# Neighbourhood attention on 8-column query tiles, with values and gates projected partly beside the head that uses them

## The chip, the cores and the metric

One core of one Trainium2 chip runs the whole program in one launch. The metric is the device time of that launch in microseconds (us), as the median of several runs. The engines are named as in the profile: PE is the matrix engine (PEld its weight loads, which overlap its products), DVE the vector engine, ACT the scalar engine, POOL the engine that here casts weights and issues the accumulating DMAs, SP the engine that issues the other DMAs.

## What is computed

A two-layer encoder on 1024 prompt tokens (16 rows x 64 columns) and 256 sample tokens (4 x 64), width 1024, in float32. The change touches only layer 0, the neighbourhood attention:

```python
proj = h @ w_in                                   # h: RMS-normed tokens
q, k, v, g = jnp.split(proj, 4, axis=-1)          # 16 heads of 64
# a query (r, c) sees 8 rows x 16 columns of keys around it; the window is
# clamped at the edges of the grid, and a per-head 2-D bias is added
s = jnp.where(mask, s + bias, NEG_INF)
p = jax.nn.softmax(s, axis=-1)
o = p @ v
return (o * jax.nn.silu(g)) @ w_out
```

Layer 1 (a gated DeltaNet) and the final norm follow, and are the same in both kernels.

## The kernel before

The tokens of the prompt are kept column after column: token index = 16 * column + row, so eight columns are 128 tokens, called a strip. Every product of float32 numbers that has to be exact is made of rounded parts: `wh` and `wl` are the high and the low part of a weight, `XH` and `XL` of the input, `KH` and `KL` of the keys, `ph` and `pl` of the probabilities. A projection is 24 products for each block of tokens (8 steps of the width, three pairs of parts; line 1108), with blocks of 512, 512 and 256 tokens. Values are projected token-major, by strip, with 24 products of 256 columns each (line 1124).

Per head h, `attention` is a generator that emits the head's steps. The prompt is cut into four tiles j of 16 columns (256 queries). In a tile, the queries are split by rows into two groups of 8 rows x 16 columns, and each group is scored against 12 key rows x 32 columns = 384 keys (`ROWS`, `SLAB`). The scores of one group are two products of 384 columns into `S` (lines 279 and 280). `softmax` (lines 224 to 227) adds the bias and takes the extreme (DVE), exponentiates and sums (ACT), takes the reciprocal and scales (DVE). The probabilities stand in tiles of 16 rows x 32 columns in which the four unseen key rows are zeros. `pv` turns them, four 128x128 transposes for two strips (line 238), rounds them to `ph` (ACT, line 241) and `pl` (DVE, line 242), and multiplies each of the four strips of values with 256 query columns, once for `ph` and once for `pl` (line 254). Lines 259 to 261 gate the result into `O`. The sample is a fifth tile with two strips.

So one head makes per prompt tile 4 score products of 384 columns, 8 transposes (4 strips x 2 groups) and 8 value products of 256 columns (4 strips x 2 parts). With the sample that is 20 score products, 36 transposes and 36 value products.

While head h is in `attention`, the projections for the next head run beside it. `Side` holds the order, written out by hand: every projection product advances a clock by its columns (`tick`), and a generator is stepped when the clock has passed the delay that it last yielded; `until` steps it without the clock until a condition holds, and `drain` empties it. The scheduler of the language keeps this as the priority, and may put a later instruction that is ready ahead of one that isn't. Beside head h run the query and key projection of head h + 1 (`qk_head`), after an odd head also the gates of the next two heads (`g_pair`, 3 blocks), and after every fourth head the values of the next four heads (`v_quad`, 10 strips). The loop is

```python
side.add(attention(h, qkk, V, G, O), 8000)
if h < 15:
    qkk = qk_head(h + 1, side)
    if h % 2:     G = g_pair((h + 1) // 2, side)
    if h % 4 == 3: V = v_quad((h + 1) // 4, side)
side.drain()
```

Weights pass through one raw buffer and three buffers each for `wh` and `wl` (`load_w`): a load by SP, a cast on POOL, a negated copy on ACT, and an accumulating DMA issued by POOL. The bias is loaded by SP, three times 384 KB for each head into two buffers. The PSUM banks are three for projections, two for `S`, two for `pt` (the transposes) and one for `O` of line 254. After head 15 the out-projection reads the heads' outputs back from memory.

Of the kernel before, what the change touches and what calls it, by code (L numbers as in the profile page):

```python
# [8 lines left out]
F32 = mybir.dt.float32  # L9
# [11 lines left out]
SLAB = [0, 8, 24, 32]  # L21
ROWS = [(0, 12), (4, 12)]
# [14 lines left out]
def layer0(ctx, tc, a, h1_out):  # L37
# [77 lines left out]
    def v_quad(q, side):  # L115
        nonlocal wv
        wv = load_v(tc, a, q)
        V = {}
        for s in range(10):
            side.until(lambda: done[4 * q - 1] > (0, 1, 1, 2, 3, 3, 3, 3, 4, 4)[s])  # L120
            V[s] = v_strip(s, token_major(s, side))
        return V

# [51 lines left out]
    with st:  # L175
# [5 lines left out]
        def qk_head(h, side=None):  # L181
# [4 lines left out]
            for b, (t0, n) in enumerate(BLK):  # L186
# [5 lines left out]
                if t0 < NP:  # L192
                    qv = Q[:, :NP].rearrange("p (g c r) -> p c g r", g=2, r=8)[:, t0 // 16:t0 // 16 + 32]
                    tq = t.rearrange("p (c g r) -> p c g r", g=2, r=8)
                else:
                    qv, tq = Q[:, c], t[:, :n]
                nc.scalar.activation(qv[0:64], tq[0:64], AF.Copy)
                nc.scalar.activation(KH[64:128, c], t[64:128, :n], AF.Copy, scale=0.125)
                nc.vector.tensor_sub(qv[64:128], tq[0:64], qv[0:64])
# [6 lines left out]
        def g_pair(p, side=None):  # L206
            wh, wl = load_w(tc, a, a["w_g"][p])
            G = []
            for b, (t0, n) in enumerate(BLK):
# [3 lines left out]
                proj(nc, ps, wh, wl, XH, XL, b, side)  # L213
                t = ap.tile([128, 512], F32, name="t", bufs=2)[:, :n]
                nc.vector.tensor_mul(t, ps, rb[:, t0:t0 + n])
                G.append(ap.tile([128, n], F32, name=f"G{b}"))
                nc.scalar.activation(G[b], t, AF.Tanh, scale=0.5)
                nc.vector.scalar_tensor_tensor(G[b], G[b], 1.0, t, op0=OP.add, op1=OP.mult)
            return G
# [9 lines left out]
        def pv(strips, hh, Od, Gv, t1v):  # L229

            O = ps_o.tile([128, 256], F32, name="O")
            ns = len(strips)

            def turned(s0):
                pt = ps_t.tile([128, 2, 256], F32, name="pt")
                for u in range(2):
                    for g in range(2):
                        nc.tensor.transpose(pt[:, u, 128 * g:128 * g + 128], strips[s0 + u][1][g], ident)  # L238
                ph = ap.tile([128, 2, 256], F32R, name="ph", bufs=2)
                pl = ap.tile([128, 2, 256], F32R, name="pl", bufs=2)  # L240
                nc.scalar.activation(ph, pt, AF.Copy)
                nc.vector.tensor_sub(pl, pt, ph)
                return ph, pl

            ts = []
            for s0 in range(0, ns, 2):
                ts.append(turned(s0))
                yield 800
            for s0 in range(0, ns, 2):
                ph, pl = ts[s0 // 2]  # L250
                for i, p in enumerate((ph, pl)):
                    for u in range(2):
                        v = strips[s0 + u][0][:, hh, :, :].rearrange("p a b -> p (a b)")
                        nc.tensor.matmul(O, v, p[:, u, :], start=(s0 + u + i == 0), stop=(s0 + u + i == ns))  # L254
                    yield 800
# [5 lines left out]
            nc.vector.tensor_mul(Od[b:b + 64], t1v(t1)[b:b + 64], Gv[b:b + 64])  # L261

        def attention(h, qkk, V, G, O):
            Q, KH, KL = qkk
            g3 = lambda t: t[:, :NP].rearrange("p (c r) -> p c r", r=16)
            g4 = lambda t, j: t[:, 256 * j:256 * j + 256].rearrange("p (c g r) -> p g c r", g=2, r=8)
            bts = {}

            def scores(j):
                if j != 2:  # L270
                    bts[j] = ap.tile([128, 768], F32, name="bias", bufs=2)
                    nc.sync.dma_start(bts[j], a["bias_p"][h, (0, 1, 1, 2)[j]])
                bt = bts[1 if j == 2 else j]
                s0 = SLAB[j]
                Pt = []
                for g, (r0, nr) in enumerate(ROWS):
                    S = ps_s.tile([128, 512], F32, name="S")[:, :nr * 32]
                    q = Q[:, 512 * g + 128 * j:512 * g + 128 * j + 128]
                    nc.tensor.matmul(S, q, g3(KH)[:, s0:s0 + 32, r0:r0 + nr], start=True, stop=False)
                    nc.tensor.matmul(S, q, g3(KL)[:, s0:s0 + 32, r0:r0 + nr], start=False, stop=True)  # L280
                    p = P[g][j % 2]
                    b = bt[:, 384 * g:384 * g + 384]
                    cr = lambda v: v.rearrange("p (c r) -> p c r", c=32)
                    softmax(cr(S), cr(b), p[:, :, r0:r0 + nr])
                    Pt.append(p)
                    yield 800
                strips = [(V[s0 // 8 + s], [p[:, 8 * s:8 * s + 8, :].rearrange("p c r -> p (c r)") for p in Pt])
                          for s in range(4)]
# [1068 lines left out]
```

## Time and profile before

| | |
|---|---|
| median of 3 runs | 2426.49 us (2420.15 to 2427.59) |
| the profiled execution | 2429.32 us, span 2427.6 us |
| PE busy | 2281.3 us, 94% of the span |
| PEld, DVE, ACT, POOL busy | 81%, 68%, 51%, 23% |
| granted PE clock, mean | 0.964 |
| first scores of head 0 to the end of head 15's attention | 80.8 to 707.2 us |

The busy time of an engine is a share of the span; the products overlap in PE's pipeline, so a product's duration in a row is longer than the time by which it delays the next one. That time is read from the starts of successive products. The stages behind 707 us (the rest of the out-projection, the DeltaNet, its out-projection and the last norm) are the same code in both kernels.

### The profile page before, as it was taken

Reading aid. Unit: us, or ns where it says so; the run is one execution under the profiler, and the core shown is the slowest. Engines: PE = TensorE matmul, PEld = TensorE weight load, DVE = VectorE, ACT = ScalarE, POOL = GpSimd, SP = SyncE. Lnnn points to the kernel's source line nnn. Section 1 sums busy time; section 2 is a strip of 40 time slices with the busy share of each in tenths; the row PEclk is TensorE's granted clock in tenths of the full one; section 3 lists DMA queues with packets and bytes.
Section 4 is the critical chain, followed back from the end, with each engine's and each line's share of the span. In section 5 each row is a group of like instructions: output and inputs, shape, how many; then the busy total and the mean of one; then the engine's idle time right before and its main releaser. Section 6 shows DMA issues by size and latency. Waiting matters only on the chain.

```text
span 2427.6 us, 37431 instructions
## 1 busy us (share of the span) xinstructions
PE 2281.3 (94%) x13462; PEld 1977.7 (81%) x13462; DVE 1642.4 (68%) x3858; ACT 1241.4 (51%) x2772; POOL 568.6 (23%) x666
## 2 busy tenths in 40 slices
PE   8999999999999698999999999999998899887996
PEld 7889888889778588888988989888777777676886
DVE  5674874784773677867868678694788888843233
ACT  6553553554662543444344443444777777754333
POOL 2000101001110521232223222233444444310100
PEclk9999999999999798989999999999999999988998
DMA  6452534443564333424443444435343334467762
GB/s 182 111 126 75 136 106 105 120 117 89 169 179 135 85 89 95 120 78 120 119 121 85 114 120 119 121 77 160 97 112 104 104 107 117 147 187 225 169 166 87
DMA packets 154649, 297.07 MB, mean 122 GB/s; under 512 B 46304, under 2 KB 83168, under 8 KB 154464
## 3 DMA queue, kind: packets, MB, share of 16 engines
q1 hardware_dynamic: 137760, 233.86, 31.5%
q0 software_dynamic: 16704, 60.82, 13.8%
q8 instruction: 106, 1.74, 0.3%
q14 instruction: 79, 0.65, 0.1%
HBM read 219.26 MB, written 64.88 MB: 117 GB/s over the span
## 4 chain that ended last, share of the span: by engine, by line
PE 63%; DVE 19%; issue 9%; DMA 5%; ACT 3%; POOL 1%; SPq 1%; DVEq 0%; ACTq 0%; POOLq 0%
PE mm L1108 26%; PE mm L1124 11%; PE O L254 3%; DVE X L564 3%; DVE tmp L562 3%; PE k L864 2%; PE k L873 2%; PE pt L238 2%; DVE acc L447 2%; PE u L839 2%; PE o L839 2%; PE o L884 2%; DMA wl<-w_go 1%; PE m L590 1%; PE S L280 1%
## 5 line engine op out<-in xcount | busy, mean ns | idle before, releaser
L1108 PE MATMUL mm<-xh,wh 128*128 128x512 f32 (+1 forms) x1536 | 560.0, 365 | 6.6 <-ACT wh L1060 5.9
L1108 PE MATMUL mm<-xh,wl 128*128 128x512 f32 (+1 forms) x1536 | 557.5, 363 | 6.1 <-DMA wl<-w_qkv 2.5
L1108 PE MATMUL mm<-xl,wh 128*128 128x512 f32 (+1 forms) x1536 | 562.2, 366 | 0.0
L1108 PEld LDWEIGHTS mm<-xh,wh 128*128 128x128 f32 x1536 | 295.3, 192 | 38.4 <-ACT wh L1060 6.4
L1108 PEld LDWEIGHTS mm<-xh,wl 128*128 128x128 f32 x1536 | 294.8, 192 | 37.8 <-DMA wl<-w_qkv 2.7
L1108 PEld LDWEIGHTS mm<-xl,wh 128*128 128x128 f32 x1536 | 295.4, 192 | 29.8 <-issue 0.5
L1124 PE MATMUL mm<-wh,xh 128*128 128x256 f32 x960 | 281.5, 294 | 4.4 <-DVE z L473 4.4
L1124 PE MATMUL mm<-wl,xh 128*128 128x256 f32 x960 | 281.4, 293 | 0.5 <-DVE wl L1062 0.5
L1124 PE MATMUL mm<-wh,xl 128*128 128x256 f32 x960 | 280.2, 292 | 0.3 <-POOL xl L66 0.3
L447 DVE SCALAR_TENSOR_TENSOR acc<-raw,cw,acc 128x1282 f32<-128x1282 f32 x128 | 201.0, 1570 | 61.8 <-ACT acc L445 60.3
L1124 PEld LDWEIGHTS mm<-wh,xh 128*128 128x128 f32 x960 | 187.7, 196 | 9.0 <-DVE z L473 4.8
L1124 PEld LDWEIGHTS mm<-wl,xh 128*128 128x128 f32 x960 | 188.0, 196 | 4.1 <-issue 2.3
L1124 PEld LDWEIGHTS mm<-wh,xl 128*128 128x128 f32 x960 | 187.9, 196 | 3.3 <-issue 1.7
L1108 PE MATMUL mm<-yh,wl 128*128 128x512 f32 (+1 forms) x384 | 143.3, 374 | 27.4 <-DMA wl<-w_go 26.7
L1060 ACT ACTIVATE wh<-wraw 128x1024 fp32r<-128x1024 f32 x94 | 99.1, 1055 | 125.3 <-PE mm L1108 51.8
L1108 PE MATMUL mm<-yh,wh 128*128 128x512 f32 (+1 forms) x384 | 142.1, 371 | 1.7 <-ACT wh L1060 1.7
L1108 PE MATMUL mm<-yl,wh 128*128 128x512 f32 (+1 forms) x384 | 142.5, 372 | 0.1
L1058 POOL CAST wh<-wraw 128x1024 fp32r<-128x1024 f32 x30 | 31.7, 1056 | 472.3 <-PE mm L1108 375.7
L1064 ACT ACTIVATE wl<-wraw 128x1024 fp32r<-128x1024 f32 x116 | 121.9, 1052 | 29.7 <-PE mm L1108 11.4
L860 POOL TENSOR_TENSOR Al<-A,Ah 128x128 fp32r<-128x128 f32 x160 | 76.0, 481 | 175.2 <-ACT Ah L859 163.2
L1108 PEld LDWEIGHTS mm<-yh,wl 128*128 128x128 f32 x384 | 76.7, 200 | 40.2 <-DMA wl<-w_go 28.5
L450 ACT ACTIVATE th<-acc 128x1282 f32<-128x1282 f32 x32 | 40.8, 1275 | 121.0 <-DVE acc L447 121.0
(325 smaller groups left out, 5307.9 us busy)
## 6 DMA issues: line engine op xcount, KB each, us to landing
bias<-bias_p SPq DMA_DIRECT2D x48, 384.0 KB, 3.1
wraw<-w_qkv SPq DMA_DIRECT2D x32, 512.0 KB, 4.2
wl<-w_qkv POOLq DMA_DIRECT2D x32, 512.0 KB, 7.3
qkv_spill<-th SPq DMA_DIRECT2D x32, 512.0 KB, 2.7
wraw<-w_go SPq DMA_DIRECT2D x32, 512.0 KB, 5.9
wl<-w_go POOLq DMA_DIRECT2D x30, 512.0 KB, 7.9
z_spill<-z SPq DMA_DIRECT2D x80, 128.0 KB, 1.7
z<-z_spill SPq DMA_DIRECT2D x80, 128.0 KB, 2.1
```

Source lines behind the costliest of these rows:

```text
L238: nc.tensor.transpose(pt[:, u, 128 * g:128 * g + 128], strips[s0 + u][1][g], ident)
L254: nc.tensor.matmul(O, v, p[:, u, :], start=(s0 + u + i == 0), stop=(s0 + u + i == ns))
L447: nc.vector.scalar_tensor_tensor(acc, r[:, i:i + m], cw[:, f, i:i + 1], acc, op0=OP.mult, op1=OP.add)
L562: nc.vector.tensor_mul(tv, N[:, 0:c, c:c + 1].to_broadcast([128, c, n]), X[:, c:c + 1, c + 1:32].to_broadcast([128, c, n]))
L564: nc.vector.tensor_add(X[:, 0:c, c + 1:32], X[:, 0:c, c + 1:32], tv)
L839: self.tc.nc.tensor.matmul(ps, w[x], v[y], start=(first and i == 0), stop=(i == 2))
L860: nc.gpsimd.tensor_sub(As[d][1], A[:, d, c], As[d][0])
L864: nc.tensor.matmul(pk, kT[:, cc[d]], S[c0, d], start=True, stop=True)
L1060: nc.scalar.activation(wh, raw, AF.Copy)
L1064: nc.scalar.activation(wl, raw, AF.Copy, scale=-1.0)
L1108: nc.tensor.matmul(ps, w[:, k, :], x[k][b], start=(k == 0 and i == 0), stop=(k == KD - 1 and i == 2))
L1124: nc.tensor.matmul(ps, x[k][b][:, cc], w[:, k % 4, :], start=(k == 0 and i == 0), stop=(k == KD - 1 and i == 2))
```

## The change

- A query tile is 8 whole columns (16 rows x 8 columns = 128 queries, one strip), m = 0 to 7. It is scored against the strips m - 1, m and m + 1 with all 16 key rows: 384 keys, 256 for m = 0 and 7. The bias is one table of 896 columns for each head, loaded once (448 KB); the zeros in the probabilities and the strided views are gone.
- Two tiles make a pair (256 queries). Strips m and m + 1 are seen by both tiles and keep products of 256 columns; strips m - 1 and m + 2 are seen by one tile each and get products of 128 columns. A pair in the middle has 6 transposes, one at an edge 5.
- The order of a pair's steps becomes scores of this pair, value products of the pair before, transposes of this pair. Before it was scores of the next tile, transposes of this one, its products.
- The gates and values of the next heads are divided: after an odd head only gate block 0 (after every fourth head also block 1 and the value strips 0 to 3); the rest is projected beside the even head that uses it, before the next `qk_head`. A generator waits in `products` until the gates and strips that it needs have been made.
- Even heads start 2000 columns into the side work instead of 8000, and the delays of a head are multiplied by 1.7, 0.9, 1.15 or 1.7.

The core of the diff:

```diff
-    def v_quad(q, side):
+    def v_quad(q, V, strips, side):
         nonlocal wv
-        wv = load_v(tc, a, q)
-        V = {}
-        for s in range(10):
+        if not V:
+            wv = load_v(tc, a, q)
+        for s in strips:
...
-                if t0 < NP:
-                    qv = Q[:, :NP].rearrange("p (g c r) -> p c g r", g=2, r=8)[:, t0 // 16:t0 // 16 + 32]
...
-                nc.scalar.activation(qv[0:64], tq[0:64], AF.Copy)
+                nc.scalar.activation(Q[0:64, c], t[0:64, :n], AF.Copy)
...
-        def g_pair(p, side=None):
-            wh, wl = load_w(tc, a, a["w_g"][p])
-            G = []
-            for b, (t0, n) in enumerate(BLK):
+        def g_pair(p, G, blocks, side=None):
+            nonlocal wg
+            if not G:
+                wg = load_w(tc, a, a["w_g"][p])
+            for b in blocks:
...
+        def turned(units):
+            ts = []
+            for us in (units[:2], units[2:]):
...
+                for u, parts in enumerate(us):
+                    for s, q0, blocks in parts:
+                        for i, blk in enumerate(blocks):
+                            o = q0 + 128 * i
+                            nc.tensor.transpose(pt[:, u, o:o + 128], blk, ident)
+                            n += 1
...
+                nc.scalar.activation(view(ph), view(pt), AF.Copy)
+                nc.vector.tensor_sub(view(pl), view(pt), view(ph))
...
+        def pv(units, ts, V, hh, Od, Gv):
+            O = ps_o.tile([128, 256], F32, name="O")
+            order = [0, *range(2, len(units)), 1]
+            for i in range(2):
+                for u in order:
+                    p = ts[u // 2][i]
+                    for s, q0, blocks in units[u]:
+                        qs = slice(q0, q0 + 128 * len(blocks))
+                        v = V[s][:, hh, :, :].rearrange("p a b -> p (a b)")
+                        nc.tensor.matmul(O[:, qs], v, p[:, u % 2, qs], start=(i == 0 and u == 0),
+                                         stop=(i == 1 and u == 1))
+                yield 1600
...
+            bt = ap.tile([128, 896], F32, name="bias", bufs=2)
+            nc.sync.dma_start(bt, a["bias_p"][h])
+            def scores(p):
+                own = {}
+                for m in (2 * p, 2 * p + 1):
+                    k0, k1 = max(m - 1, 0), min(m + 2, 8)
+                    n = 128 * (k1 - k0)
+                    S = ps_s.tile([128, 512], F32, name="S")[:, :n]
+                    q = Q[:, 128 * m:128 * m + 128]
+                    nc.tensor.matmul(S, q, KH[:, 128 * k0:128 * k1], start=True, stop=False)
+                    nc.tensor.matmul(S, q, KL[:, 128 * k0:128 * k1], start=False, stop=True)
...
-            todo = yield from scores(0)
-            for j in range(1, 5):
-                after = yield from (scores(j) if j < 4 else scores_s())
-                yield from todo
-                done[h] += 1
-                todo = after
-            yield from todo
+            last = None
+            for j in range(5):
+                units = yield from (scores(j) if j < 4 else scores_s())
+                if last:
+                    yield from products(*last)
+                else:
+                    yield 3200
+                ts = yield from turned(units)
+                last = j, units, ts
+            yield 1600
+            yield from products(*last)
...
-            side.add(attention(h, qkk, V, G, O), 8000)
+            G = nG if h % 2 == 0 else G
+            V = nV if h % 4 == 0 else V
+            side.add(attention(h, qkk, V, G, O), 2000 if h % 2 == 0 else 8000, (1.7, 0.9, 1.15, 1.7)[h % 4])
+            side.tick(0)
+            p, q = (h + 1) // 2, (h + 1) // 4
+            if h % 2 == 0:
+                g_pair(p, G, [b for b in range(3) if b not in G], side)
+                v_quad(q, V, [s for s in range(10) if s not in V], side)
             if h < 15:
...
                 qkk = qk_head(h + 1, side)
-                if h % 2:
-                    G = g_pair((h + 1) // 2, side)
+            if h % 2 and h < 15:
+                nG = {}
+                g_pair(p, nG, [0], side)
                 if h % 4 == 3:
-                    V = v_quad((h + 1) // 4, side)
+                    nV = {}
+                    v_quad(q, nV, range(4), side)
+                    g_pair(p, nG, [1], side)
             side.drain()
```

More of the change, by code (lines that the diff above doesn't have):

```diff
@@ L227, in softmax @@
             nc.vector.tensor_scalar(Pv, Pv, mx[:, 2:3], None, op0=OP.mult)
[L229 to L234, printed above, removed]
+        def turned(units):
+            ts = []
+            for us in (units[:2], units[2:]):
+                if not us:
+                    break
                 pt = ps_t.tile([128, 2, 256], F32, name="pt")
-                for u in range(2):
-                    for g in range(2):
-                        nc.tensor.transpose(pt[:, u, 128 * g:128 * g + 128], strips[s0 + u][1][g], ident)
@@ L239, in turned @@
                 ph = ap.tile([128, 2, 256], F32R, name="ph", bufs=2)
                 pl = ap.tile([128, 2, 256], F32R, name="pl", bufs=2)
[L241 to L247, printed above, removed]
-                yield 800
[L249 to L255, printed above, removed]
+                n = 0
@@ L267, in attention @@
[L267 to L285, printed above, removed]
+            bt = ap.tile([128, 896], F32, name="bias", bufs=2)
@@ new lines, in attention @@
+            nc.sync.dma_start(bt, a["bias_p"][h])
[8 more added lines that the diff above has]
+                    nc.tensor.matmul(S, q, KL[:, 128 * k0:128 * k1], start=False, stop=True)
+                    P = ap.tile([128, 384], F32, name="P", bufs=4)
+                    b0, _ = BIAS[0 if m == 0 else 2 if m == 7 else 1]
+                    softmax(S, bt[:, b0:b0 + n], P[:, :n])
+                    for s in range(k0, k1):
+                        own[s, m] = P[:, 128 * (s - k0):128 * (s - k0) + 128]
@@ L286, in scores @@
                     yield 800
[L287 to L290 removed]
+                m = 2 * p
+                edge = [(s, 128 * i, [own[s, m + i]]) for s, i in ((m - 1, 0), (m + 2, 1)) if (s, m + i) in own]
+                return [[(s, 0, [own[s, m], own[s, m + 1]])] for s in (m, m + 1)] + [edge]
@@ L301, in scores_s, with products @@
                     softmax(S[:, g], bs[:, g], Ps[:, g])
[L302 to L313 removed]
+                yield 1600
+                return [[(8 + s, 0, [Ps[:, g, 128 * s:128 * s + 128] for g in range(2)])] for s in range(2)]
+            def products(j, units, ts):
+                while not (j // 2 in G and all(s in V for us in units for s, _, _ in us)):
+                    yield 400
+                g = G[j // 2][:, 256 * (j % 2):256 * (j % 2) + 256]
+                yield from pv(units, ts, V, h % 4, O[:, 256 * j:256 * j + 256], g)
+                done[h] += 1
+            last = None
[7 more added lines that the diff above has]
+                last = j, units, ts
+            yield 1600
+            yield from products(*last)
             if h % 2 and h < 15:
```

62 lines of the change are left out of this document (25 added, 37 removed).

## The prediction

> **What bounds the kernel now.** I read the page's totals first, then the stretches of the attention stage head by head, then who waits for whom in it, then the order in time on PE. The page says that PE is busy 94% of the span. That is an average; the stretches say it for the stage that is changed (heads 0, 1, 3 and 14, then the whole; the columns are length, busy time of PE, PEld, DVE, ACT and POOL with instruction counts, granted clock, DMA share, GB/s).
>
> ```profile
> span 2427.6 us, 37431 instructions
> 80.80:107.30 26.50, 26.39 (x161) 22.02 (x160) 22.56 (x65) 17.12 (x40) 1.91 (x2) 1.00 0.47 108
> 107.30:149.00 41.70, 41.14 (x241) 34.81 (x240) 29.81 (x78) 20.75 (x47) 3.82 (x4) 1.00 0.47 128
> 175.60:246.10 70.50, 69.94 (x481) 63.60 (x480) 34.60 (x88) 26.54 (x58) 5.73 (x6) 1.00 0.36 94
> 647.80:680.70 32.90, 28.23 (x160) 23.53 (x159) 28.30 (x70) 26.52 (x60) 14.09 (x12) 0.95 0.75 220
> 80.80:707.20 626.40, 615.09 (x3832) 529.53 (x3831) 433.40 (x1163) 330.24 (x741) 65.78 (x66) 1.00 0.46 117
> ```
>
> The heads last from 26.5 to 70.5 us, very uneven, but PE is busy in 98% or more of the first three and of the whole, at the full clock; the light heads have DVE at 22.56 of 26.50 us, high and still behind PE. Head 14, light as head 0, has a hole (28.23 of 32.90). So PE's work is what the stage costs, and a gain is counted in the time by which a product delays the next one, which only the order in time shows:
>
> ```profile
> 81.62 0.34 PE L279 MATMUL S<-KH,Q 128*128 128x384 f32 x1
> 81.80 0.34 PE L280 MATMUL S<-KL,Q 128*128 128x384 f32 x1
> 81.97 0.40 PE L1108 MATMUL mm<-xh,wh 128*128 128x512 f32 x1
> ...
> 84.65 1.00 PE L238 MATMUL pt<-ident,P 128*128 128x128 f32 x7
> 85.41 0.47 PE L1108 MATMUL mm<-xh,wl 128*128 128x512 f32 x1
> 85.72 0.40 PE L1108 MATMUL mm<-xh,wh 128*128 128x512 f32 x1
> 86.01 0.50 PE L254 MATMUL O<-ph,V 128*128 128x256 f32 x2
> 86.35 0.39 PE L1108 MATMUL mm<-xl,wh 128*128 128x512 f32 x1
> 86.58 0.40 PE L1108 MATMUL mm<-xh,wl 128*128 128x512 f32 x1
> 86.82 0.42 PE L254 MATMUL O<-pl,V 128*128 128x256 f32 x2
> 87.08 0.39 PE L1108 MATMUL mm<-xh,wh 128*128 128x512 f32 x1
> ...
> 971.73 1.30 PE L610 MATMUL m<-WT,B 128*128 128x64 f32 x10
> 972.84 0.48 PE L1108 MATMUL mm<-xh,wh 128*128 128x512 f32 x1
> ```
>
> and, from the chain of waits, a run of products of 256 columns:
>
> ```profile
> 213.83 27.38 PE mm L1124 x228
> ```
>
> Seven transposes take 85.41 - 84.65 = 0.76 us, 109 ns each. A product of 512 columns takes 0.23 us (86.35 to 86.58), two of 384 0.35 (81.62 to 81.97; 176 ns each), one of 256 27.38 / 228 = 120 ns. A value product of 128 columns does not exist before. Its nearest row is that of line 610: ten products of 64 columns, each with weights of 128 columns of its own, take 1.11 us, 111 ns each, hardly less than 256 columns. So a narrow product seems to be paid by its weight load. I take 111 ns; the upper end is 120 (256 columns), the lower one 65, the straight line through 512 and 256 columns.
>
> **The change part by part.** The counts of instructions that PE has in the stage come from the groups:
>
> ```profile
> L238 PE MATMUL pt<-ident,P 128*128 128x128 f32 x512 | 80.8, 275 | 4.8 <-DVE P L227 4.8
> L238 PE MATMUL pt<-ident,Ps 128*128 128x128 f32 x64 | 11.1, 273 | 0.0
> L280 PE MATMUL S<-KL,Q 128*128 128x384 f32 x128 | 43.3, 339 | 1.3 <-DMA KL<-KL 1.3
> L254 PE MATMUL O<-ph,V 128*128 128x256 f32 x288 | 64.2, 304 | 0.1
> ```
>
> 1. Transposes. (512 + 64) / 16 = 36 for each head; after it 6 + 6 + 5 + 5 + 4 = 26, counting the two blocks of each of the two shared strips, one for each single strip, and the sample's four. 160 fewer at 109 ns: **-17.4 us**.
>
> 2. Scores. 16 products of 384 columns become 12 of 384 and 4 of 256 (tiles 0 and 7); the sample is as it was. 64 products at 176 - 120 = 56 ns: **-3.6 us**. That the keys are read in one piece and not by 12 of 16 rows is put at nothing: 384 columns at 176 ns are hardly slower than their share of 512 (172).
>
> 3. Value products. Before, 2 x 288 / 16 = 36 of 256 columns. After it, 20 of 256 (16 and the sample's 4) and 12 of 128 (4 + 4 + 2 + 2): 36 x 120 = 4.32 us against 20 x 120 + 12 x 111 = 3.73. Over 16 heads **-9.4 us**, -7.7 at 120 ns and -18.2 at 65. [...]
>
> 4. The order of the steps. Before, value products follow their transposes directly and wait for the rounding; transposes come a whole tile after their scores. After the change it is the other way round.
>
> ```profile
> PEld O L254 <- DVE pl L242: 17.4, 65, 0.5
> PEld O L254 <- ACT ph L241: 16.9, 62, 0.5
> PEld pt L238 <- DVE P L227: 7.1, 10, 3.8
> ...
> L224 DVE CUSTOM_DVE_ANT_0 P<-S,bias 128x384 f32<-128x384 f32 x128 | 70.1, 549 | 29.9 <-PE S L280 22.6 <-DMA wraw<-w_g 6.0
> L225 ACT ACTIVATE P<-P,mx 128x384 f32<-128x384 f32 x128 | 78.4, 613 | 25.9 <-DVE mx L224 23.9 <-DVE O L261 0.6
> L225 ACT ACTIVATION_READ_ACCUMULATOR P<-P,mx 128x1 f32 x128 | 23.9, 187 | 0.0
> L226 DVE RECIPROCAL mx<-mx 128x1 f32<-128x1 f32 x160 | 24.3, 153 | 2.8 <-ACT P L225 2.5
> L227 DVE TENSOR_SCALAR P<-P,mx 128x384 f32<-128x384 f32 x128 | 55.3, 433 | 1.3
> ```
>
> 127 of the bursts of value products had their weight load wait, 0.27 us in the mean, part of it under a running product. In the order above the `ph` burst costs 0.34 us and the product ahead of it 0.29, together 0.16 more than 0.24 + 0.23; the `pl` burst and its forerunner 0.26 + 0.24, 0.03 more. At 0.1 us each that is 12.7 us, which goes, since two score steps and their side products now lie between rounding and use. What is late next is the softmax: from scores to turned probabilities 549 + 613 + 187 + 153 + 433 = 1.94 us of work, and 2.7 us with the gaps between engines (scores given out by 81.97, their transposes from 84.65). The cover from the second tile's scores to the transposes is 800 + 1600 + 1600 columns times the pace, rounded up to whole products. At pace 0.9 that is 2 + 3 + 3 products of 0.23 us, with the eight value products between, 1.84 + 0.93 = 2.8 us, just even; at 1.15 and 1.7 it is 3.2 us or more. So waits are likely in heads 1, 5, 9 and 13, and in heads 0 and 15, part or all of which runs with no side work: 6 x 9 = 54 transposing bursts at 0.16 us, the larger loss above, 8.6 us. Together **-4 us**; ends -12.7 (no new wait) and +5 (54 bursts at 0.33 us, twice that, less 12.7).
>
> 5. Evening out. No term, because nothing waits in the light heads that it would free. It is cover: without it, item 1 to 3 would bring PE in a light head to 26.5 - 1.9 = 24.6 us, near DVE's 22.56. DVE is cut too: `pl` and `ph` are made for 5 bursts of 512 columns and 4 narrow ones instead of 9.
>
> 6. Weights. Values 0 to 3 now start one gate block after `qk_head`, and the second half of their weights needs the buffer that `qk_head` frees. The accumulating DMA behind that takes long:
>
> ```profile
> wl<-w_v POOLq DMA_DIRECT2D x6, 512.0 KB, 8.4
> ```
>
> ```profile
> L1064 ACT ACTIVATE wl<-wraw 128x1024 fp32r<-128x1024 f32 x28 | 29.7, 1060 | 22.9 <-DMA wraw<-w_g 10.9 <-PE mm L1108 9.1 <-PE mm L1124 2.5
> ```
>
> The copy and the DMA make 1.06 + 8.4 = 9.5 us (the cast on POOL runs beside). The cover is gate block 0 (24 x 0.23 = 5.5 us), the first 12 products of three strips, one for each bank (36 x 0.12 = 4.3 us), and the attention steps between. I put it at nothing; without the strips the wait would be 4 us in heads 3, 7 and 11, +12 us in all. Behind it on POOL and SP stand only the next weights, due 17 us of value products later.
>
> 7. Bias. One load of 448 KB for three of 384. SP and the DMA engines (share 0.46) are not what ends any wait of weight here; nothing.
>
> 8. Head 14 loses 32.9 - 26.5 = 6.4 us, because ACT takes `xh<-xl` conversions ahead of the softmax and stands for their loads, and the transposes stand for it:
>
> ```profile
> ACT xh L349 <- DMA xl<-o_spill: 3.8, 2, 2.1
> PE pt L238 <- DVE P L227: 3.3, 1, 3.3
> ```
>
> The last readers of the inputs are still the products of `qk_head` 15, so the loads come at the same place; I leave it unchanged, ends -6 (by then most of head 14 is done) and 0.
>
> Sum: -17.4 - 3.6 - 9.4 - 4 = **-34.4 us** against the profiled execution's 2429.3, so 2395. The median of the runs stands 2.8 us below the profiled execution: **2392 us**. Differences below 0.3% (7 us) count as no change, as the runs before spread over 7.4 us.
>
> **The rivals.** (a) More than that: the waits at the value products go, no new ones come, and head 14's hole closes: -30.4 - 12.7 - 6.4 = -49, or -58 with 65 ns; about 2373. For it speaks that the scheduler puts ready products ahead of an unready burst; against it that such bursts waited 127 times all the same. (b) Half of it is given back: the second half of the value weights is late by 4 us three times (item 6) and item 4 comes out at +5: -30.4 + 12 + 5 = -13, 2413. (c) Slower: the softmax becomes the wait in each of the 9 transposing bursts of all heads. It decides from 30.4 + 12.7 = 43 us over 144 bursts, 0.30 us each; at 0.4 us it is +14, 2440. The place is PE's weight load for the transposes, behind DVE's scaling. ACT and DVE also carry the projections' evacuations, 0.6 us each, in the same queues, so a softmax that comes behind two of them is that late. [...] Against it: at pace 1.15 and 1.7 the cover is above 3 us, and side products can be put in front. (d) The change does nothing measurable: only if the transposes were free under other work, which 98% busy contradicts; or if (b) and half of (c) meet.
>
> **How the numbers follow.** Forecast (-20 to -44) 0.60; (a) 0.14; (b), -7 to -20, 0.12; (d) 0.06; (c) 0.08. Faster 0.86, same 0.06, slower 0.08. The range that leaves out 2 in 10 goes from 2370, near (a)'s end, to 2416, just beyond (b); the forecast alone is 2382 to 2406.
>
> **What would show it.** 416 transposes (352 and 64), 320 score products of which 128 have 256 columns, and 512 value products of which 192 have 128 columns, the latter 111 ns apart (item 3; 65 would make the price by weight load wrong). Head stretches near 25, 31, 34, 47 and 45 us, the stage about 590 us, PE still 98% busy in each. The waits of line 254's loads for `ph` and `pl` gone (item 4); those of the transposes for DVE's scaling below 10 us, mostly in the heads of pace 0.9. If they are 40 us, (c) was right; if PE waits for `wl<-w_v` in heads 3, 7 and 11, (b). If the stages behind the attention move by more than 3 us, the forecast fails for a reason that it does not hold.

## The result, and the profile after

The changed kernel is a little slower. Its median is 2441.03 us (7 runs, 2435.72 to 2448.11) against 2427.78 us of the kernel before in the same comparison (7 runs, 2420.15 to 2433.03): a ratio of 1.0052, with an interval of 1.0035 to 1.0069. The forecast was 2392 us, range 2370 to 2416; it is wrong, and outside its range. The profiled execution took 2438.63 us.

The page's first line for the kernel after, and the stretches of its attention stage: heads 0 to 4, head 14, and the whole. The columns are those of the prediction (length; busy time of PE, PEld, DVE, ACT, POOL; granted clock; DMA share; GB/s).

```profile
span 2436.9 us, 36859 instructions
76.00:103.40 27.40, 26.92 (x160) 22.89 (x158) 20.64 (x64) 16.14 (x41) 3.25 (x4) 1.00 0.44 101
103.40:135.80 32.40, 29.91 (x167) 24.89 (x166) 25.08 (x73) 17.12 (x45) 2.07 (x2) 0.95 0.35 91
135.80:178.60 42.80, 38.47 (x225) 33.25 (x224) 29.15 (x78) 20.25 (x47) 3.82 (x4) 1.00 0.41 102
178.60:220.70 42.10, 41.37 (x274) 37.15 (x275) 25.13 (x72) 17.48 (x45) 1.91 (x2) 1.00 0.29 76
220.70:274.40 53.70, 49.67 (x342) 45.64 (x340) 31.02 (x80) 24.59 (x54) 7.71 (x8) 1.00 0.45 105
637.50:684.80 47.30, 40.78 (x223) 34.49 (x222) 37.24 (x84) 31.45 (x69) 16.25 (x14) 0.93 0.56 161
76.00:706.60 630.60, 589.38 (x3618) 514.26 (x3617) 419.74 (x1161) 309.56 (x740) 66.89 (x67) 0.98 0.39 98
```

PE has 25.7 us less to do in the stage (615.09 to 589.38), yet the stage isn't shorter. PE is busy 93% of it and no longer 98%, with 41 us of holes instead of 11, and the granted clock is 0.98 and no longer 1.00. The stage also begins earlier (76.0, not 80.8 us), because head 0 now starts sooner in the side work; so the mark to compare is where the attention ends, the end of the last value product of head 15: 704.6 us before, 706.6 after.

The waits say what the holes are. First who waits for whom on PE and PEld in this stage, kernel after (us in total, times, longest):

```profile
PE S L282 <- DMA KH<-KH: 16.9, 6, 3.5
PE S L283 <- DMA KL<-KL: 6.0, 4, 1.8
PE S L301 <- DVE mx L218: 6.3, 9, 1.8
PE pt L239 <- DVE P L221: 6.0, 7, 3.2
PEld O L259 <- ACT ph L243: 4.7, 16, 0.5
PEld O L259 <- DVE pl L244: 3.2, 11, 0.8
```

Then the same engine's key waits before, which are one line in all:

```profile
PE S L280 <- DMA KL<-KL: 1.3, 1, 1.3
```

The waits at the value products went as forecast (17.4 + 16.9 us of PEld before, 7.9 after), and the softmax did not become the bound. But PE now stands 16.9 + 6.0 = 22.9 us for two transfers: the copies of the rounded keys `KH` and `KL` from partitions 64 to 127 to partitions 0 to 63, at the first scores of a head. Nothing in the prediction had a price for them.

They land late, and not only because less work is left to cover them. The DMA issues of this stage (count, KB each, median us from issue to landing), first before, then after:

```profile
KH<-KH SPq DMA_DIRECT2D x15, 320.0 KB, 3.2
KL<-KL SPq DMA_DIRECT2D x15, 320.0 KB, 4.9
```

```profile
KH<-KH SPq DMA_DIRECT2D x15, 320.0 KB, 7.6
KL<-KL SPq DMA_DIRECT2D x15, 320.0 KB, 9.0
```

The same transfers of 320 KB take 2.4 and 1.8 times as long. The order in time at the end of a key projection shows why. Kernel after, the end of the projection for head 3 (start, us, engine, line; the bracket is idle time and its releaser), and the first scores that use it:

```profile
169.06 1.07 ACT L1082 ACTIVATE wl<-wraw 128x1024 fp32r<-128x1024 f32 x1 [0.55 <-PE mm L1126]
...
170.19 0.33 SPq L1072 DMA_DIRECT2D wraw<-w_v  x1
170.43 0.86 POOL L1083 DMA_DIRECT2D wl<-w_v  x1 [0.35 <-ACT Q L190]
170.46 0.42 ACT L191 ACTIVATE KH<-t 64x256 fp32r<-64x256 f32 x1
170.90 0.47 SPq L195 DMA_DIRECT2D KH<-KH  x1
171.47 0.54 SPq L196 DMA_DIRECT2D KL<-KL  x1
...
178.57 0.56 PE L282 MATMUL S<-KH,Q 128*128 128x256 f32 x2 [2.94 <-DMA KH<-KH]
```

The same place in the kernel before (ACT alone, end of the projection for head 1):

```profile
100.65 0.41 ACT L198 ACTIVATE KH<-t 64x256 fp32r<-64x256 f32 x1
101.09 1.06 ACT L1064 ACTIVATE wl<-wraw 128x1024 fp32r<-128x1024 f32 x1
```

When the last product of the projection has run, two things become possible: the negated copy `wl` of the next weights (their buffer is free) and the conversions of the last key block. Before, ACT took the conversions first, in all of heads 1 to 13, and the accumulating weight load followed the key copy by 1.4 us. After, the weight copy comes first in all thirteen. ACT has less to do in the stage (309.56 us busy, 330.24 before) and in twelve of them comes to this point 0.3 us or more before DVE's scaling has ended, for which the conversions wait; here it had even stood idle for 0.55 us. That this is why the order turned is a reading of the order in time; what the order costs is tested below. The copy frees `wraw`, so a raw weight load of 512 KB is issued at 170.19 and an accumulating one of 512 KB at 170.43; the key copies follow at 170.90 and 171.47, 0.5 to 1.3 us behind 1 MB of weights, and the first scores stand 2.94 us for them. In heads 14 and 15, where no weight load stands just ahead, the `KH` copy lands in 4.2 and 3.2 us.

The kernel before had one such copy too, in a place where it cost nothing. Its `KH` copy for head 0, issued at 65.40 us, 0.5 us behind an accumulating weight load and 0.7 behind a raw one, took 8.2 us to land, the longest of its sixteen; their median is 3.2.

A second loss follows from the holes. The clock in stretches of 1 us behind the key wait of head 1 (same columns), and products of 512 columns in the same place (the first pair at the low clock, the second at the full one):

```profile
106.00:107.00 1.00, 1.00 (x4) 0.81 (x4) 0.98 (x4) 0.51 (x2) 0.00 (x0) 0.50 0.08 31
...
110.00:111.00 1.00, 1.00 (x6) 0.78 (x6) 1.00 (x3) 0.53 (x2) 0.00 (x0) 1.00 0.00 0
...
105.59 0.39 PE L283 MATMUL S<-KL,Q 128*128 128x256 f32 x1 [1.83 <-DMA KL<-KL]
108.13 0.63 PE L1126 MATMUL mm<-xl,wh 128*128 128x512 f32 x1
108.55 0.63 PE L1126 MATMUL mm<-xh,wl 128*128 128x512 f32 x1
109.82 0.39 PE L1126 MATMUL mm<-xh,wl 128*128 128x512 f32 x1
110.05 0.39 PE L1126 MATMUL mm<-xh,wh 128*128 128x512 f32 x1
```

Behind the hole the clock is granted at 0.50 for about 3.4 us, and products of 512 columns start 0.42 us apart instead of 0.23. Summed over the stage in stretches of 1 us, one less the granted clock, this comes to 12.0 us after (five dips: four at key waits, about 106, 304, 344 and 611 us, the longest of them 6.8 us, and one in head 14) and 1.7 us before (one, in head 14).

So the end of the attention can be reckoned up. PE's work -30, by the prices of the prediction's items 1 to 3; the order of steps about 0 (below); key waits +22.9 - 1.3 = +21.6, or +23.6 when the time between successive starts on PE beyond each product's usual slot is summed (25.0 less 1.4); lower clock +12.0 - 1.7 = +10.3. Together +2 to +4, where the profiled pair shows 706.6 - 704.6 = +2.0.

### The profile page after: what moved, and what is told of

Read it like the earlier page. It is cut to its first block, busy times and chain, and to the rows that moved or that the text cites. A ratio compares the mean times of both kernels' runs of the same rounds, so it can differ in the third digit from the quotient of the medians.

```text
span 2436.9 us, 36859 instructions
## 1 busy us (share of the span) xinstructions
PE 2256.7 (93%) x13238; PEld 1963.3 (81%) x13238; DVE 1629.6 (67%) x3858; ACT 1221.2 (50%) x2772; POOL 568.1 (23%) x662
## 3 DMA queue, kind: packets, MB, share of 16 engines
q1 hardware_dynamic: 133152, 222.33, 29.5%
## 4 chain that ended last, share of the span: by engine, by line
PE 58%; DVE 18%; issue 9%; DMA 8%; ACT 6%; POOL 1%; SPq 1%; DVEq 0%; ACTq 0%; POOLq 0%
PE mm L1126 24%; PE mm L1142 11%; DVE X L582 3%; DVE tmp L580 3%; PE k L882 2%; PE k L891 2%; PE o L902 2%; DVE acc L465 2%; PE u L857 2%; PE o L857 2%; DMA KH<-KH 2%; PE O L259 2%; DMA KL<-KL 2%; PE pt L239 1%; PE m L608 1%
## 5 line engine op out<-in xcount | busy, mean ns | idle before, releaser
L1082 ACT ACTIVATE wl<-wraw 128x1024 fp32r<-128x1024 f32 x116 | 121.9, 1051 | 21.6 <-PE mm L1126 9.5
L219 ACT ACTIVATE P<-P,mx 128x384 f32<-128x384 f32 (+1 forms) x128 | 74.9, 585 | 82.5 <-DVE mx L218 80.3
```

Source lines behind the costliest of these rows:

```text
L219: nc.scalar.activation(Pv, Pv, AF.Exp, scale=-1.0, bias=mx[:, 0:1], accum_out=mx[:, 1:2])
L1082: nc.scalar.activation(wl, raw, AF.Copy, scale=-1.0)
```

## The experiments

The theory: the key copies, queued behind weights, take back the gain; the rivals are the new order of steps, the softmax, and the division of gates and values. Each ratio is to the kernel before, run beside it, with a 95% interval. "Attention ends" is the last value product of head 15 in the profiled execution; that mark is 704.6 and 701.1 in two executions of the kernel before, and 706.6 and 711.2 in two of the kernel after.

**korder**: the kernel after, with every `wl` copy held behind the last key conversion traced so far.

```diff
-                nc.scalar.activation(KH[64:128, c], t[64:128, :n], AF.Copy, scale=0.125)
+                a["k_conv"] = nc.scalar.activation(KH[64:128, c], t[64:128, :n], AF.Copy, scale=0.125)
...
-        nc.scalar.activation(wl, raw, AF.Copy, scale=-1.0)
+        k = a.get("k_conv") if a.get("hi") else None
+        with tc.issue_after(k.ins) if k else ExitStack():
+            nc.scalar.activation(wl, raw, AF.Copy, scale=-1.0)
```

> The changed kernel with one order pinned: the negated weight copy on ACT goes behind the last key conversion, so that the key copies (KH and KL to the other 64 partitions) are issued ahead of the weight loads. Theory K (the saved PE work was given back at the heads' first scores, which wait for key copies that land 7.6 and 9.0 us after their issue instead of 3.2 and 4.9, since they queue behind 1 MB of weights): landing back to 3 to 5 us, PE's waits for KH and KL from 23 us to below 6, the time from 2441 to about 2420. Theory S (the new order of steps exposes the softmax, which is what costs): no key wait matters, 2441 within 4.

Measured: 2582.9 us, 1.0644 (1.0623 to 1.0664); attention ends 858.1. The edit does more than it was meant to. It holds the copy of all weights that are fetched early behind the key projection before them, so that PE waits for weights, 44.8 us for those of the gates, 40.9 for those of the query and key projections and 13.4 for those of the values (waits of PE in the stage):

```profile
PE mm L1128 <- DMA wl<-w_g: 44.8, 8, 6.5
PE S L282 <- DMA KH<-KH: 25.5, 7, 3.7
```

The key copies did land in 3.3 and 4.8 us, as expected, but the waits for them did not fall: PE stood 25.5 us for `KH` all the same. So neither the time nor the waits speak for the theory here. The edit is made again, narrower, in korder2.

**kblock**: the kernel after, with the keys copied per block, each as soon as it is converted. Four fifths of the keys (1024 of 1280 tokens) are then under way before the last block's products have run.

```diff
-            nc.sync.dma_start(KH[0:64, :].bitcast(F32), KH[64:128, :].bitcast(F32))
-            nc.sync.dma_start(KL[0:64, :].bitcast(F32), KL[64:128, :].bitcast(F32))
+                nc.sync.dma_start(KH[0:64, c].bitcast(F32), KH[64:128, c].bitcast(F32))
+                nc.sync.dma_start(KL[0:64, c].bitcast(F32), KL[64:128, c].bitcast(F32))
```

> The changed kernel with the key copies issued by block (six for each head instead of two), so that the prompt's keys are copied while the sample's are still projected. K: the first scores need the first block alone, which is there 8 us earlier; waits for KH and KL nearly gone, 2441 to about 2417, a little better than with the order alone. S: 2441 within 4, or slower by SP's additional issues.

Measured: 2396.21 us, 0.9870 (0.9853 to 0.9888), 33 us below the kernel before. The stage:

```profile
76.00:668.90 592.90, 574.23 (x3592) 505.36 (x3591) 419.01 (x1161) 309.16 (x740) 66.32 (x67) 0.99 0.42 104
```

No row of the waits names a key copy any more, 6.8 us are lost to the lower clock, and the attention ends at 668.9. The key waits (22.9 us) and the lower clock (5 us less) make up most of the 37.7 us by which it ends earlier than in the kernel after. Another part, up to 6 us, is work put off: up to that mark 26 fewer projection products have run, of at most 0.23 us each. The last of the three copies, which carries the sample's keys alone, still lands late, and the two of twice its size do not:

```profile
KH<-KH SPq DMA_DIRECT2D x32, 128.0 KB, 2.2
...
KH<-KH SPq DMA_DIRECT2D x16, 64.0 KB, 6.8
```

In before_kblock, further down, the 48 copies of `KH`, 64 and 128 KB, land in 1.9 us at the least and 2.2 in the median. So the edit leaves the last copy nearly as late as the 320 KB of the kernel after (6.8 against 7.6 us); it gets four fifths of the keys out ahead of it. That the weights still stand ahead of that last copy is a reading of its landing. The time is within 4 us of the forecast, and two moved lines lay between. That it comes so near is in part chance, since the forecast had no term for the lower clock.

**kchip**: no copies at all; ACT and DVE write the lower halves too.

```diff
+                nc.scalar.activation(KH[0:64, c], t[64:128, :n], AF.Copy, scale=0.125)
...
-            nc.sync.dma_start(KH[0:64, :].bitcast(F32), KH[64:128, :].bitcast(F32))
-            nc.sync.dma_start(KL[0:64, :].bitcast(F32), KL[64:128, :].bitcast(F32))
+                nc.vector.scalar_tensor_tensor(KL[0:64, c], t[64:128, :n], 0.125, KH[64:128, c],
+                                               op0=OP.mult, op1=OP.subtract)
```

> The changed kernel without the key copies: ACT and DVE write both halves of KH and KL themselves, 3 more instructions each for a head (about 1.7 us on either). K: no wait for a key copy is left, about 2417, the same as by block. S: DVE and ACT carry more in front of the softmax, so 2441 or slower, to 2450.

Measured: 2411.55 us, 0.9931 (0.9912 to 0.9950); attention ends 679.6. The key waits are gone here too, and most of the loss with them, which speaks for the transfer. Some 11 us of the stage are lost again against kblock (the attention ends at 679.6 and not 668.9). The two engines of the softmax do the copying: from 76 to 707 us DVE is busy 457.57 us here and 432.90 in kblock, ACT 350.78 and 325.33. That this is where the 11 us go is a reading.

**tiles**: the new tiles alone, with the old order of steps and undivided gates and values.

```diff
+            def tail(j, units):
+                ts = yield from turned(units)
+                yield from products(j, units, ts)
...
-                if last:
-                    yield from products(*last)
-                else:
-                    yield 3200
-                ts = yield from turned(units)
-                last = j, units, ts
-            yield 1600
-            yield from products(*last)
+                if todo:
+                    yield from todo
+                todo = tail(j, units)
+            yield from todo
...
-            side.add(attention(h, qkk, V, G, O), 2000 if h % 2 == 0 else 8000, (1.7, 0.9, 1.15, 1.7)[h % 4])
...
+            side.add(attention(h, qkk, V, G, O), 8000)
...
```

> The 8-column tiles alone: the order of a head's steps, the undivided gates and values, the delays and the single pace are those of before. Both theories expect the PE saving of 30 us to show here, K because the attention of the head before still covers the copies, S because the softmax has a whole tile of cover: 2428 to about 2398. If it stays above 2415, the saving itself was priced wrongly (products of 128 columns or the transposes).

Measured: 2437.23 us, 1.0043 (1.0026 to 1.0060); attention ends 708.8. The lighter tiles alone bring out the loss (DMA issues, then waits):

```profile
KH<-KH SPq DMA_DIRECT2D x16, 320.0 KB, 8.1
...
PE S L282 <- DMA KH<-KH: 14.8, 7, 2.8
```

Neither the new order nor the division is needed for it. Both theories had expected 2398 us here; the one on the key copies was wrong in that the attention of the head before does not cover them any more. Here, too, the copies land late, `KH` in 8.1 us in the median and 3.2 at the least. The reading is that a head's attention, being shorter, leaves ACT free too early and PE without other work; no run changes this alone.

**korder2**: the narrower order. Only the weight load that takes the buffers just freed by `qk_head` (the third load behind it) has its `wl` copy held behind that projection's last key conversion. Nothing is taken from the prefetch of the others.

```diff
+            mine = a["loads"]
...
-                nc.scalar.activation(KH[64:128, c], t[64:128, :n], AF.Copy, scale=0.125)
+                a["k_conv"][mine] = nc.scalar.activation(KH[64:128, c], t[64:128, :n], AF.Copy, scale=0.125)
...
+    a["loads"] = a.get("loads", 0) + 1
...
-        nc.scalar.activation(wl, raw, AF.Copy, scale=-1.0)
+        k = a["k_conv"].get(a["loads"] - 3) if a.get("hi") else None
+        with tc.issue_after(k.ins) if k else ExitStack():
+            nc.scalar.activation(wl, raw, AF.Copy, scale=-1.0)
```

> The changed kernel with a narrower pin than before: only the weight load that takes the buffers which a query and key projection has just freed has its negated copy on ACT placed behind that projection's last key conversion; all other loads keep their prefetch. Theory K: the key copies are issued ahead of the weights and land in 3 to 5 us, PE's waits for KH and KL fall from 23 us to below 8, and the time from 2441 to about 2420; what is left is that they land 4 to 5 us after the projection and the next head starts 3.6 us after it. Theory S (the order of steps): 2441 within 4.

Measured: 2411.23 us, 0.9917 (0.9893 to 0.9940); attention ends 677.1. DMA issues and waits:

```profile
KH<-KH SPq DMA_DIRECT2D x16, 320.0 KB, 3.2
KL<-KL SPq DMA_DIRECT2D x16, 320.0 KB, 4.7
...
PE S L283 <- DMA KH<-KH: 0.7, 1, 0.7
```

The copies are issued at the same point of the program with the same bytes; only what stands ahead of them has changed, and they land in 3.2 and 4.7 us, nearly as in the kernel before. That shows the cause, the weights issued ahead, apart from the copying itself. It brings back less than kblock does (0.9917 against 0.9870). The attention ends 8.2 us later than there, and up to that mark 26 more projection products have run, some 6 us of it; what else the difference in time is stays open.

**before_kblock**: the control, the edit of kblock in the kernel before.

```diff
-            nc.sync.dma_start(KH[0:64, :].bitcast(F32), KH[64:128, :].bitcast(F32))
-            nc.sync.dma_start(KL[0:64, :].bitcast(F32), KL[64:128, :].bitcast(F32))
+                nc.sync.dma_start(KH[0:64, c].bitcast(F32), KH[64:128, c].bitcast(F32))
+                nc.sync.dma_start(KL[0:64, c].bitcast(F32), KL[64:128, c].bitcast(F32))
```

> Control: the kernel before with key copies by block, nothing else. There PE waits for key copies 1.3 us in all, so K expects no change, 2429 within 4. If it gains 20 us or more, the copies by block do something else than end these waits, and their gain in the changed kernel is no evidence for K.

Measured: 2432.46 us, 1.0001 (0.9987 to 1.0015). In the kernel before, the copies were hidden and moving them is worth nothing. The same edit is worth 44 us in the one kernel (1.0052 less 0.9870 of 2430) and nothing in the other, so the 33 us of kblock against the kernel before belong to the new tiles and what came with them.

**tiles_kblock, order_kblock, split_kblock**: kblock with parts of the rest taken back. tiles_kblock is tiles, order_kblock has the new order of steps but undivided gates and values, split_kblock has the division but the old order of steps; all three copy the keys by block. Their diffs are those of tiles (the first hunk takes the order back, the second the division) and kblock.

> The 8-column tiles alone (order, division, delays and pace as before) with key copies by block. K: the saving of 30 us that the tiles alone did not show at 2437 was held back by 17 us of waits for KH and KL; it comes out at about 2410, and, as the light heads stay light, 10 to 15 us above the whole change with copies by block (2396). If it stays above 2425, the tiles cost something that is not a key wait.

> 8-column tiles, the new order of a head's steps and key copies by block, with gates and values undivided, delays of 8000 and pace 1. If dividing the gates and values is worth nothing (as the prediction put it), the same as the whole change with copies by block, 2396 within 5. If evening out pays once PE has less to do, 2405 or more. Theory S expects the softmax to stand in the light heads above all: 2410 or more with waits of the transposes for DVE above 20 us.

> 8-column tiles with key copies by block, the divided gates and values with their delays and paces, but the old order of a head's steps (scores of the next pair, transposes, value products). With the waits for rounding back (about 20 us of PE's waits at the value products, as with the tiles alone and copies by block) and those for the softmax gone: between the tiles alone with copies by block (2416) and the whole change with copies by block (2396), about 2408. If the division does all the work, 2398 or less; if the order does, 2413 or more.

Measured: tiles_kblock 2415.65 us, 0.9941 (0.9918 to 0.9964); order_kblock 2402.09, 0.9877 (0.9859 to 0.9895); split_kblock 2403.26, 0.9909 (0.9892 to 0.9925). Waits of PEld and PE in the stage, first in tiles_kblock:

```profile
PEld O L259 <- ACT ph L243: 37.1, 93, 0.8
```

The same view of order_kblock:

```profile
PE pt L239 <- DVE P L221: 13.8, 25, 3.1
PE S L301 <- DVE mx L218: 0.8, 2, 0.6
```

Of split_kblock:

```profile
PEld O L259 <- ACT ph L243: 29.8, 64, 4.8
```

And of kblock:

```profile
PE pt L239 <- DVE P L221: 5.5, 4, 3.3
PE S L301 <- DVE mx L218: 7.2, 9, 2.8
```

The order of steps changes one wait for the other, as item 4 had it: without it PEld stands for `ph`, with it for the softmax. The new order is worth 13.6 us between tiles_kblock and order_kblock, and some 9 us between split_kblock and kblock (0.9909 less 0.9870 of 2430). The division more than halves the transposes' waits for the softmax (13.8 against 5.5 us), but the sample's scores then wait for it instead (0.8 against 7.2 us), for the score bank that its first step has yet to read. So little is gained: 0.9877 against 0.9870, which the intervals do not tell apart. Under the old order of steps the division gives 0.9941 against 0.9909, where they overlap too.

**after2, before2**: both kernels once more, for a second trace.

> The changed kernel once more, unaltered, for a second execution with a trace. If the time after the attention (1730 us in its first trace, 1723 and 1733 in two traces in which the attention ended at the same time) belongs to the change, it is 1730 again within 2; if it is scatter of the executions, anything from 1722 to 1733, with the attention ending at 706 within 3 all the same.

> The kernel before once more, unaltered, for a second trace. The changed kernel's two traces have 1730 us behind the attention, the kernel before has 1723 in its one trace, and with key copies by block 1733 although its attention ends within 2 us of before. If 1723 belongs to the kernel before, it is 1723 again within 2, and some 7 us of the changed kernel's loss lie behind the attention by the place at which the later stages start; if executions scatter by that much, it is anything from 1722 to 1733.

Measured: after2 2447.54 us, 1.0081 (1.0066 to 1.0096); before2 2433.04 us in one run, beside 2433.76 for the kernel before. The key waits repeat (`after2`):

```profile
PE S L282 <- DMA KH<-KH: 21.4, 9, 4.0
```

The two traces also bear on the stages behind the attention, which are the same code. (One less the granted clock is summed as above.) From the end of the attention to the end of the span they last 1723.0 us before, 1730.1 in before2, 1730.3 after and 1730.1 in after2. Of these, 86.5, 93.9, 93.6 and 97.1 us are lost to a granted clock below 1. So the 7.3 us between the profiled executions of before and after goes with the clock, and occurs between two executions of the kernel before as well; in kblock the same part lasts 1729.8 us with 85.0 lost, so the clock isn't all of it. The mark is not the same point of the program either: up to it PE has run 9 more projection products after than before, some 2 us, and 17 fewer in kblock, some 4 us. Whether the part of the 13 us between the medians that the attention does not explain (it ends 2 us later in one pair of traces and 10 in the other, where after2, at 711.2, missed the 706 within 3 that were expected) is more than this stays open.

**pin14**: kblock, and beside it the conversions of the out-projection's inputs (`OH`, on ACT) held behind the last exponential of head 14.

```diff
-            nc.scalar.activation(Pv, Pv, AF.Exp, scale=-1.0, bias=mx[:, 0:1], accum_out=mx[:, 1:2])
+            a["exp"] = nc.scalar.activation(Pv, Pv, AF.Exp, scale=-1.0, bias=mx[:, 0:1], accum_out=mx[:, 1:2])
...
+            if h == 14:
+                last = a["exp"]
...
-                nc.scalar.activation(OH[k][b], t, AF.Copy)
+                with tc.issue_after(last.ins):
+                    nc.scalar.activation(OH[k][b], t, AF.Copy)
```

> The changed kernel with key copies by block, and the conversions of the stored head outputs on ACT placed behind the last exponential of head 14. If the 8 us by which head 14 is longer than its PE work come from those conversions standing in front of the softmax, head 14 gets 5 to 8 us shorter; head 15 has less of the out-projection ready to fill it and gives back some. 2396 to about 2392; unchanged within 4 if head 15 gives back all of it.

Measured: 2395.19 us, 0.9873 (0.9853 to 0.9893); attention ends 664.7. Head 14 in kblock, then in pin14:

```profile
604.30:643.30 39.00, 34.03 (x195) 29.00 (x194) 29.66 (x74) 24.68 (x55) 9.99 (x8) 0.91 0.54 167
```

```profile
603.50:635.20 31.70, 31.45 (x195) 27.68 (x194) 25.64 (x72) 21.04 (x50) 5.86 (x4) 1.00 0.65 197
```

Head 14 loses its hole (39.0 to 31.7 us, clock 0.91 to 1.00), and head 15 takes back 3.9 us (25.6 to 29.5), where the conversions now stand. The attention ends 4.2 us earlier; in the time the two kernels are not told apart. They and order_kblock are the fastest here; korder2, kchip, split_kblock and tiles_kblock beat both kernels as well, by less.

## Why the prediction was wrong

**The step that failed** is item 7 together with the sum. Item 7 said of SP and the DMA engines that they "are not what ends any wait of weight here; nothing", and looked at the bias alone. The key copies have no term anywhere. They had been hidden by a condition of the kernel before (by the reading above, ACT busy with the attention at the moment a key projection ends, and attention left over on PE while they ran), and items 1 to 3 removed just this cover, as the run tiles shows (14.8 us of waits for `KH`, 2437.23 us). The runs showed in its place 22.9 us of PE standing for the key copies and 10.3 us more of lower clock, of which 8.5 us came behind such waits; together they are as much as the 30 us that PE's work fell by. The rows that could have told were there: one wait of 1.3 us for `KL`, one transfer in fifteen already at the limit, and the one `KH` copy issued behind weights, for head 0, which took 8.2 us. Asking of every transfer on the path "what hides it, and does the change shorten that" would have found a price between nothing and, if nothing covers it, the 3.2 us or more of its landing in each of 15 heads. When the weights would be issued was reckoned for their own readers (item 6), and not for what they push aside.

- **Items 1 to 3, PE's work: right.** The counts are exact, from the rows of a tile (minimum, median and maximum ns, then first and last start):

```profile
L239 PE MATMUL pt<-ident,P x352: 270/272/477, 80.5 to 700.9; 128*128 128x128 f32 x176
L239 PE MATMUL pt<-ident,Ps x64: 270/272/329, 102.9 to 704.4; 128*128 128x128 f32 x64
L282 PE MATMUL S<-KH,Q x128: 276/337/579, 76.0 to 692.6; 128*128 128x384 f32 x96, 128*128 128x256 f32 x32
```

- **The price of a narrow value product (item 3): right in the sum.** Kernel after, a burst of 256, 128, 128 and 256 columns and the product behind it, in order of time:

```profile
92.16 0.62 PE L259 MATMUL O<-ph,V 128*128 128x256 f32 x4
92.62 0.28 PE L1126 MATMUL mm<-xh,wh 128*128 128x256 f32 x1
```

The four take 92.62 - 92.16 = 0.46 us, and 2 x 120 + 2 x 111 ns is 0.46; 0.46 is also the median of all 54 such bursts in this trace.

- **Item 4: right in what goes and what comes, near nothing in the sum.** Waits at the value products fell from 34.3 to 7.9 us of PEld, of which about 12 us were time of PE, as forecast. Between successive starts on PE, waits for the softmax rose from 5.8 to 15.0 us (+9), and the sample's scores stand 6.3 us instead of 3.8 for `mx` (line 301, three of the waits 1.7 to 1.8 us long), which was not foreseen. Together about 0 where -4 was taken, within the ends given. That the order is worth 9 to 14 us in the runs with copies by block is no contradiction: there the other side is the new tiles in the old order, whose waits of PEld for `ph` alone are 37.1 us and not the 16.9 of the kernel before.

- **Item 5, no term for the evening out: not refuted.** It moves softmax waits from the transposes to the sample's scores, and order_kblock and kblock are not told apart in time.

- **Item 6: right.** No wait for `wl<-w_v` appears at heads 3, 7 and 11. Rival (b) did not occur; but the same weights, issued early, did their harm one queue further, at the keys.

- **Item 8: right.** Head 14 kept its hole, and pin14 (on top of kblock) shows that the conversions were its cause.

- **The list of stretches.** Near 25, 31, 34, 47 and 45 us were named; after it they are 27.4, 32.4, 42.8, 42.1 and 53.7, with the key waits and low clock inside. kblock has 27.2, 29.1, 35.3, 44.8 and 50.8 (48.2 and 48.1 in heads 8 and 12), and a stage of 592.9 against the 590 named: what the prediction reckoned, it reckoned well on the whole.

- **Rival (c)** gave the right side and nearly the right time, 2440 us, by the wrong mechanism: the waits of the transposes for DVE's scaling are 6.0 us on PE, not 40.

- **The stages behind the attention** moved by 7.3 us in the first pair of traces, more than the 3 us that were named as a sign of another reason. The kernel before moves as far between its own two traces, so the pair does not show that the change did it.

## What to carry to other kernels

When an engine's work is cut, list every transfer whose landing was covered by that work, and price each as if the cover were gone; a row with one small wait among fifteen hidden transfers is a warning, not a zero. Look also at what the freed engine will take first, because an engine that comes free a microsecond earlier can let a megabyte of prefetch go ahead of the one small copy that the path needs (here ACT came to the weight copy 0.3 us or more before the scaling had ended, and the `KH` copy landed in 7.6 us and not 3.2). Issue small, urgent transfers in pieces as their data comes to be (kblock, 0.9870 where the kernel after has 1.0052), and hold prefetches behind them (korder2, 0.9917).

## What the runs showed of the hardware

A hole on PE can cost nearly as much again as its own length: 1.83 us of waiting up to 105.59 was followed by 3.413 us at half the clock, 1.7 us lost. The length of a hole does not settle it alone. Holes of 1.83 and 1.66 us (up to 302.88) were followed by such a stretch in the kernel after, one of 2.94 us (at 178.57) was not, and in after2 one of 2.88 us at the same scores was. Of the five stretches at half the clock in this stage, three last 3.413 us and two 6.827.

In the clock records of the kernel after, the five falls to half clock, at 105.85, 303.82, 344.78, 611.02 and 662.22 us, lie 197.97, 40.96, 266.24 and 51.20 us apart: 58, 12, 78 and 15 times 3.413 us, to within 0.03. No such stretch follows four key waits of over 2 us (2.94, 2.34, 2.49 and 3.19 us, up to 178.57, 274.36, 444.51 and 513.84), nor the 1.73 us up to 423.29; one follows the 2.42 us up to 609.84. What tells these holes apart is not shown; no run shifted a hole.

A copy of 320 KB between partitions (`KH`) lands in 3.2 us (medians of before and korder2) and in 7.6 to 8.1 us (medians of after, after2 and tiles). In heads 1 to 13 of the kernel after, 1 MB of weight loads was issued 0.5 to 1.8 us ahead of it, and it lands in 7.0 to 9.4 us; in head 15, with no weight load just ahead, in 3.2. In korder2, which holds those loads back, the longest of the sixteen copies takes 3.8 us. A fifth of the size does not help: the 64 KB of kblock take 6.8 us, where its 128 KB take 2.2.

In the burst of four value products above, the starts lie at 92.16, 92.28, 92.34, 92.45 and, for the product behind it, 92.62: 120 ns behind the first wide product, 61 and 111 behind the two narrow ones, 171 behind the second wide one. The sum is what the prices say; the parts are not, and over the 47 such bursts that stand alone the medians are the same to 2 ns.
